# Second FFN of a hybrid decoder layer: two token parts and seven block products in place of eight

## The chip, the cores and the metric

One core of one Trainium2 chip runs the whole program. The metric is device time in microseconds: the median of the runs. In the profile, PE is TensorE (PEld its weight loads), DVE is VectorE, ACT is ScalarE, POOL is GpSimd, and SP issues most of the DMAs.

## The reference

One inference step of a decoder layer on 16 meta tokens, 1024 prompt tokens and 64 sample tokens, all in float32:

```python
x = x + 0.5 * swiglu(rmsnorm(x, g1), w1, w3, w2)      # first FFN
x = x + mix(rmsnorm(x, g)) @ w_out                    # three recurrent groups
x = x + 0.5 * swiglu(rmsnorm(x, g2), w1b, w3b, w2b)   # second FFN
y = rmsnorm(x, g_final)                               # meta tokens are dropped

def swiglu(x, w1, w3, w2):
    return (silu(x @ w1) * (x @ w3)) @ w2             # 1024 -> 2816 -> 1024
```

## The kernel before

The residual x lies with features on partitions (8 blocks of 128) and tokens along the free dimension, in three token blocks of 336, 384 and 384 columns. The second FFN leaves out the 16 meta tokens, so its blocks have 320, 384 and 384. A float32 product is made of three products of the engine's reduced float32 form: `split` (L102 to L104) rounds a tensor to a high part on ACT (L103) and subtracts it on DVE for the low part (L104), and `gemm3` (L187) sums high x high, low x high and high x low in PSUM.

`ffn` goes over the 22 slices of 128 hidden features in pairs. For each slice and token block it makes the products with w1 and w3 (8 feature blocks x 3 terms, 24 matmuls each), multiplies by 1/rms (L221, L223), applies tanh and the gate (L222 to L225), splits the result (hh, hl), and then adds the product with w2 into the residual (matmul L247, DVE L249). Weights are loaded on SP in 512 KB pieces (L177) and split by `wload`.

Three phases follow each other: the input and the first FFN, the mixing, and from L1272 the second FFN with the final norm. In the mixing, the residual lies in DRAM; `w_out` of blocks 0 and 1 is part of it. Phase 3 begins with the loads of these two blocks (L1282), their scaling and splitting (`xsplit`, L124 and L125) and the sums of squares (`square`: ACT L138, POOL L139). Then w_out of block 2 is issued (matmul L187 into pwo, DVE L1290), and after it block 2 is prepared in the same way. `rsq` (L106 to L114) is 1/sqrt by some ten small DVE operations, and `rstd_bc` spreads it over partitions (L164, L165, L167).

In the last pair of slices `turn` transposes the residual (L1309, L1310), and `finish` makes the w2 products with tokens on partitions (512 columns, L1329), adds (DVE L1331), squares (ACT L1333), multiplies by the final gain (POOL L1334), applies 1/rms (ACT L1349, DVE L1351) and stores; it runs block by block between the products of that pair. Each engine works off its instructions in an order fixed at build time by a scheduler; the order of issue in the code is its priority.

## Time and profile before

| | us |
|---|---|
| median of 3 runs (2209.11 to 2211.9) | 2211.64 |
| the profiled execution, span from first to last instruction | 2210.2 |
| PE busy | 2154.1 |
| DVE busy | 1258.3 |
| ACT busy | 675.9 |
| POOL busy | 110.1 |

Busy time is the union of an engine's instructions; the granted TensorE clock has a mean of 0.990 of its full rate over the span. A stretch is to be read by itself: the shares above are means over the three phases.

### The profile page before, as it was taken

Reading aid. Unit: us, or ns where it says so; the run is one execution under the profiler, and the core shown is the slowest. Engines: PE = TensorE matmul, PEld = TensorE weight load, DVE = VectorE, ACT = ScalarE, POOL = GpSimd, SP = SyncE. Lnnn points to the kernel's source line nnn. Section 1 sums busy time; section 2 is a strip of 40 time slices with the busy share of each in tenths; the row PEclk is TensorE's granted clock in tenths of the full one; section 3 lists DMA queues with packets and bytes.
Section 4 is the critical chain, followed back from the end, with each engine's and each line's share of the span. In section 5 each row is a group of like instructions: output and inputs, shape, how many; then the busy total and the mean of one; then the engine's idle time right before and its main releaser. Section 6 shows DMA issues by size and latency. Waiting matters only on the chain.

```text
span 2210.2 us, 32814 instructions
## 1 busy us (share of the span) xinstructions
PE 2154.1 (97%) x13190; PEld 2102.0 (95%) x13190; DVE 1258.3 (57%) x2841; ACT 675.9 (31%) x1356; POOL 110.1 (5%) x176
## 2 busy tenths in 40 slices
PE   8999999999999999999998899999999999999996
PEld 7999999999999999978997798999999999999995
DVE  7444545454444467766687886654445444444537
ACT  6221111111111144645646664311111111111214
POOL 3000000000000021000000001300000000000004
PEclk9999999999999999999999999999999999999998
DMA  6011111111111125544344346211111111111202
GB/s 180 29 48 39 54 33 48 48 48 39 48 48 39 39 71 154 131 136 137 105 104 108 84 120 198 65 39 48 48 39 58 30 57 49 39 39 48 67 1 81
DMA packets 224875, 154.56 MB, mean 70 GB/s; under 512 B 40671, under 2 KB 210180, under 8 KB 224212
## 3 DMA queue, kind: packets, MB, share of 16 engines
q1 hardware_dynamic: 219932, 150.70, 23.3%
q10 hardware_dynamic: 4792, 1.78, 0.4%
q8 instruction: 103, 1.69, 0.3%
q14 instruction: 48, 0.39, 0.1%
HBM read 123.22 MB, written 29.22 MB: 69 GB/s over the span
## 4 chain that ended last, share of the span: by engine, by line
PE 89%; DVE 5%; ACT 3%; DMA 3%; issue 1%; SPq 0%; DVEq 0%; ACTq 0%
PE p L187 47%; PE p L247 22%; PE pw L187 9%; PE pwo L187 3%; PE pq L552 1%; PE pA L754 1%; DVE sl L125 1%; ACT sh L124 1%; PE p L1329 1%; PE pgt L466 0%; DVE x L249 0%; DVE rsy L114 0%; DMA sh<-in_x_prompt_dram 0%; DMA x<-xspill 0%; PE xps L1309 0%
## 5 line engine op out<-in xcount | busy, mean ns | idle before, releaser
L249 DVE SCALAR_TENSOR_TENSOR x<-p,x 128x384 f32<-128x384 f32 (+2 forms) x504 | 265.2, 536 | 304.0 <-PE p L247 302.1
L187 PE MATMUL p<-sh,whi 128*128 128x384 f32 (+2 forms) x2112 | 403.5, 329 | 0.4 <-ACT sh L124 0.4
L187 PE MATMUL p<-sl,whi 128*128 128x384 f32 (+2 forms) x2112 | 403.4, 328 | 0.0
L187 PE MATMUL p<-sh,wlo 128*128 128x384 f32 (+2 forms) x2112 | 400.6, 328 | 0.0
L187 PEld LDWEIGHTS p<-sh,wlo 128*128 128x128 f32 x2112 | 359.0, 188 | 0.0
L187 PEld LDWEIGHTS p<-sh,whi 128*128 128x128 f32 x2112 | 356.5, 188 | 1.7 <-ACT sh L124 1.4
L187 PEld LDWEIGHTS p<-sl,whi 128*128 128x128 f32 x2112 | 357.1, 188 | 0.2
L247 PE MATMUL p<-hh,whi 128*128 128x384 f32 (+2 forms) x1008 | 331.7, 329 | 1.9 <-DVE x L249 1.8
L247 PE MATMUL p<-hh,wlo 128*128 128x384 f32 (+2 forms) x1008 | 331.8, 329 | 0.0
L247 PE MATMUL p<-hl,whi 128*128 128x384 f32 (+2 forms) x1008 | 331.3, 329 | 0.0
L103 ACT CAST whi<-wraw 128x1024 fp32r<-128x1024 f32 x168 | 176.2, 1049 | 394.7 <-PE p L247 242.2
L103 ACT CAST hh<-h 128x336 fp32r<-128x336 f32 (+1 forms) x132 | 65.8, 498 | 535.4 <-DVE h L225 479.2
L104 DVE TENSOR_TENSOR wlo<-wraw,whi 128x1024 fp32r<-128x1024 f32 x168 | 205.2, 1221 | 23.3 <-ACT whi L103 19.9
L223 DVE TENSOR_TENSOR t<-p,rb 128x336 f32<-128x336 f32 (+1 forms) x132 | 71.0, 538 | 222.0 <-PE p L187 221.9
L247 PEld LDWEIGHTS p<-hh,whi 128*128 128x128 f32 x1008 | 189.7, 188 | 2.8 <-DVE x L249 2.7
L247 PEld LDWEIGHTS p<-hh,wlo 128*128 128x128 f32 x1008 | 189.3, 188 | 0.0
L247 PEld LDWEIGHTS p<-hl,whi 128*128 128x128 f32 x1008 | 189.3, 188 | 0.0
L222 ACT ACTIVATE h<-t 128x336 f32<-128x336 f32 (+1 forms) x132 | 67.4, 511 | 334.3 <-DVE t L221 334.3
L221 DVE TENSOR_TENSOR t<-p,rb 128x336 f32<-128x336 f32 (+1 forms) x132 | 70.8, 536 | 142.5 <-PE p L187 136.4
L104 DVE TENSOR_TENSOR hl<-h,hh 128x336 fp32r<-128x336 f32 (+1 forms) x132 | 71.2, 539 | 49.6 <-ACT hh L103 49.1
L187 PE MATMUL pw<-sh,whi 128*128 128x384 f32 (+1 forms) x480 | 99.2, 338 | 0.1
L187 PE MATMUL pw<-sh,wlo 128*128 128x384 f32 (+1 forms) x480 | 98.4, 337 | 0.0
(415 smaller groups left out, 2301.6 us busy)
## 6 DMA issues: line engine op xcount, KB each, us to landing
wraw<-in_ffn_w_dram SPq DMA_DIRECT2D x132, 512.0 KB
wraw<-in_w_in_dram SPq DMA_DIRECT2D x16, 512.0 KB
wraw<-in_w_out_dram SPq DMA_DIRECT2D x16, 512.0 KB
xspill<-x SPq DMA_DIRECT2D x2, 1536.0 KB
x<-xspill SPq DMA_DIRECT2D x2, 1536.0 KB
sl<-in_x_prompt_dram SPq DMA_DIRECT2D x5, 512.0 KB
wP<-m_minus_b SPq DMA_DIRECT2D x8, 256.0 KB
qk<-z_qk SPq DMA_DIRECT2D x8, 256.0 KB
```

Source lines behind the costliest of these rows:

```text
L103: S.copy(hi, x)
L104: V.tensor_tensor(lo, x, hi.bitcast(F32), OP.subtract)
L124: S.mul(hi[:, k, :n], X[:, k, :n], vc(gname, k))
L125: V.scalar_tensor_tensor(lo[:, k, :n], X[:, k, :n], vc(gname, k), hi[:, k, :n].bitcast(F32), OP.mult, OP.subtract)
L187: PE.matmul(p, wsl(ww, k), xsl(xx, k), start=i == 0, stop=i == tot - 1)
L221: V.tensor_tensor(t1, p1[:, :n], rb[b], OP.mult)
L222: S.activation(h, t1, AF.Tanh, scale=0.5)
L223: V.tensor_tensor(t3, p3[:, :n], rb[b], OP.mult)
L247: PE.matmul(p[:, :n], w[:, g, :], x[:, :n], start=i == 0, stop=i == 3 * GRP - 1)
L249: V.scalar_tensor_tensor(X[b][:, d, :n], p[:, :n], 0.25, X[b][:, d, :n], OP.mult, OP.add)
L552: PE.matmul(p[:96, h, :m], wt[:, kb, sl, 0:96], cm[:, kb, :m], start=i == 0, stop=i == len(ks) - 1)
L754: PE.matmul(p[:, a], x[:, a], y[:, a], start=True, stop=True)
```

## The change

The 1088 tokens of the second FFN are worked off in two parts, of 576 and of 512 columns (`PARTS`), one after the other, each through all 22 slices, its output included; the weights are read and split once for each part. In each part the tokens are cut into two halves of n = 288 or 256 columns, the 1024 features into two halves, and a pair of slices is two blocks of hidden features. The product of this 2x2 scheme with w1, and the one with w3, is made of seven block products (`seven`, 12 matmuls of n columns each) in place of eight. For these, `operands` forms seven combinations of the normalised blocks of x once for each part, and splits each; `weights` forms seven combinations of the weight blocks for every pair (four POOL operations at L1372, seven splits). Partial sums are read out of PSUM banks a, b and c by ACT and DVE between products, while some banks go on summing. 1/rms is now part of x's operands. The w_out of block 2 is issued at the end of the mixing and goes to DRAM; SBUF of the first two phases is freed before phase 3, whose tiles take its place.

```diff
+PARTS = [(288, [(0, 64), (64, 128), (192, 128), (320, 128), (448, 128)]), (256, [(0, 128), (128, 128), (256, 128), (384, 128)])]
+PARTS = [(288, [(0, 64), (64, 128), (192, 128), (320, 128), (448, 128)]), (256, [(0, 128), (128, 128), (256, 128), (384, 128)])]
+ORDER = (1, 6, 2, 7, 5, 4, 3)
...
-
-    # ================================================================ phase 1: input and first FFN
+        w_out((2,), out01)
...
+    front.close()
     with ExitStack() as ph:
-        for b in range(2):
-            nc.sync.dma_start(X[b], xdr2[b][:, :, skip[b] : NB[b]])
-            for k in range(8):
-                xsplit(X[b], b, k, "ffn2_norm_g")
-                square(tp, X[b], b, k)
-            rstd_bc(tp, b)
-        nc.sync.dma_start(X[2], xdr[2])
-
-        def out2(b, d, p):
-            V.tensor_tensor(X[2][:, d, :], X[2][:, d, :], p, OP.add)
-
-        w_out((2,), out2)
-        for k in range(8):
-            xsplit(X[2], 2, k, "ffn2_norm_g")
-            square(tp, X[2], 2, k)
-        rstd_bc(tp, 2)
-
...
+        X = [xp.tile([128, 8, 2 * n], F32, tag=f"x{i}", name=f"x{i}") for i, (n, _) in enumerate(PARTS)]
+        nc.sync.dma_start(X[0][:, :, 0:320], xdr2[0][:, :, 16:336])
+        nc.sync.dma_start(X[0][:, :, 320:576], xdr2[1][:, :, 0:256])
+        nc.sync.dma_start(X[1][:, :, 0:128], xdr2[1][:, :, 256:384])
+        nc.sync.dma_start(X[1][:, :, 128:512], xdr2[2])
...
+            S.activation(acc, X[i][:, 0, :], AF.Square)
+            for k in range(1, 8):
+                q = tp.tile([128, 576], F32, tag="h", name="sq", bufs=3)[:, : 2 * n]
+                S.activation(q, X[i][:, k, :], AF.Square)
+                G.tensor_tensor(acc, acc, q, OP.add)
...
+            def block(fh, th):
+                t = temp()
+                for k in range(4):
+                    S.mul(t[:, k, :], X[i][:, 4 * fh + k, th * n : th * n + n], vc(gname, 4 * fh + k))
+                V.tensor_tensor(t, t, r[:, th, None, :].to_broadcast([128, 4, n]), OP.mult)
+                return t
...
+            b11, b12 = block(0, 0), block(0, 1)
+            t1 = minus(b12, b11)
+            split(*ops[1], b11)
+            b22 = block(1, 1)
+            t3 = minus(b22, b12, b12)
+            t2 = minus(b22, t1)
+            split(*ops[6], t2)
+            b21 = block(1, 0)
+            split(*ops[2], b21)
+            for p, t in ((7, t3), (5, t1)):
+                split(*ops[p], t)
+            split(*ops[4], minus(b21, t2, b21))
+            split(*ops[3], b22)
+            return ops
...
+        def weights(w, f):
+            r = []
+            for i in range(2):
+                t = wq.tile([128, 4, 256], F32, tag="raw", name="wraw", bufs=3)
+                src = w.rearrange("(k p) f -> p k f", p=128)
+                nc.sync.dma_start(t, src[:, 4 * i : 4 * i + 4, f * 128 : f * 128 + 256])
+                r.append(t)
+            a11, a21 = r[0][:, :, 0:128], r[0][:, :, 128:256]
+            a12, a22 = r[1][:, :, 0:128], r[1][:, :, 128:256]
+            def comb(x, y, op):
+                t = wq.tile([128, 4, 128], F32, tag="ws", name="ws", bufs=4)
+                G.tensor_tensor(t, x, y, op)
+                return t
+            s1 = comb(a21, a22, OP.add)
+            s2 = comb(s1, a11, OP.subtract)
+            s3 = comb(a11, a21, OP.subtract)
+            s4 = comb(a12, s2, OP.subtract)
+            u = {}
+            for p, x in zip(ORDER, (a11, s2, a12, s3, s1, a22, s4)):
+                hi = wq.tile([128, 4, 128], F32R, tag="whi", name="whi", bufs=7)
+                lo = wq.tile([128, 4, 128], F32R, tag="wlo", name="wlo", bufs=7)
+                split(hi, lo, x)
+                u[p] = (hi, lo)
+            return u
...
+        def seven(u, ops, n, y1, y2):
+            a, b, c = bank("a"), bank("b"), bank("c")
+            s = tp.tile([128, 288], F32, tag="p1", name="p1")[:, :n]
...
+                for ww, xx in ((wh, xh), (wh, xl), (wl, xh)):
                     for k in range(4):
+                        PE.matmul(
+                            t[:, :n], ww[:, k, :], xx[:, k, :], start=first and i == 0, stop=i == 11,
+                            skip_group_check=True,
+                        )
+                        i += 1
...
+            mm(a, 1, True)
+            S.copy(s, a[:, :n])
+            mm(b, 6, True)
+            add(y1[:, h2], s, b)
+            mm(a, 2, False)
+            S.copy(y1[:, h1], a[:, :n])
+            mm(b, 7, False)
+            add(y2[:, h2], s, b)
+            mm(c, 5, True)
+            add(y2[:, h2], y2[:, h2], c)
+            mm(b, 4, False)
+            add(y2[:, h1], s, b)
+            mm(c, 3, False)
+            add(y1[:, h2], y1[:, h2], c)
...
+                G.tensor_tensor(xq, xq, gb[:m, q * 512 : q * 512 + 512], OP.mult)
...
+        for i, (n, _) in enumerate(PARTS):
+            ops = operands(i, "ffn2_norm_g")
+            for f0 in range(0, NFB, 2):
+                last = f0 + 2 == NFB
+                ys_ = {}
+                for nm in ("ffn2_w1", "ffn2_w3"):
+                    u = weights(A[nm], f0)
+                    t = [lp.tile([128, 576], F32, tag=f"c{nm[-1]}{g}", name="c")[:, : 2 * n] for g in range(2)]
+                    seven(u, ops, n, *t)
+                    ys_[nm[-1]] = t
+                u2 = halves(f0)
...
+                for d in range(8):
+                    wh, wl = (t[:, :, d % 4 * 128 : d % 4 * 128 + 128] for t in u2[d // 4])
+                    for o, m in ((0, n), (n, n)) if 2 * n > 512 else ((0, 2 * n),):
+                        p = pz_("p2")
+                        c = 0
+                        for g in range(2):
+                            hh, hl = (t[:, o : o + m] for t in hs[g])
+                            for w, x in ((wh, hh), (wh, hl), (wl, hh)):
+                                PE.matmul(p[:, :m], w[:, g, :], x, start=c == 0, stop=c == 5)
+                                c += 1
+                        xs = X[i][:, d, o : o + m]
+                        V.scalar_tensor_tensor(xs, p[:, :m], 0.25, xs, OP.mult, OP.add)
+                if last:
+                    for j, (o, m) in enumerate(PARTS[i][1]):
+                        x = lp.tile([128, 1152], F32, tag="bf", name="xt", bufs=4)[:, :1024]
+                        turned(x, i, o, m)
+                        output(i, j, o, m, x)
```

The order in which the engines' queues stand changes at three places. The first is SP, where the second FFN begins. Before, the loads of blocks 0 and 1 (x_13473, x_13474) are issued ahead of the last w_out weights:

```order
L999 DMA xspill_1_82<-stg 128x384
L177 DMA wraw<-in_w_out_dram 128x8x128
L1282 DMA x_13473<-xspill_0_81 128x8x320
L1282 DMA x_13474<-xspill_1_82 128x3072
L1287 DMA x_13475<-xspill_80 128x3072
L177 DMA wraw<-in_w_out_dram 128x8x128 x2
L177 DMA wraw<-in_ffn_w_dram 128x8x128 x4
```

In the change, the parts' loads (x_13759 for part 0, x_13760 for part 1) stand behind the stores of block 2 (xspill_2, from the last w_out products), and the FFN's weights behind them:

```order
L992 DMA xspill_2_83<-stg 128x384 x2
L1283 DMA gb<-in_final_norm_g_dram 128x1024
L1285 DMA x_13759<-xspill_0_81 128x8x320
L992 DMA xspill_2_83<-stg 128x384
L1286 DMA x_13759<-xspill_1_82 128x8x256
L1287 DMA x_13760<-xspill_1_82 128x8x128
L1429 DMA w_14180<-in_ffn_w_dram 128x2x512
L1288 DMA x_13760<-xspill_2_83 128x8x384
L1365 DMA wraw<-in_ffn_w_dram 128x4x256 x3
```

The load of the first token block moved from ahead of w_out's last weights to the end of w_out.

The second is PE at the same place; pwo are w_out's sums, p and a are those of w1 and w3. Before:

```order
L187 MATMUL pwo<-sh_12405,wlo 128x384 x5
L165 MATMUL rbp<-dg,ones 128x64
L165 MATMUL rbp<-dg,ones 128x128 x2
L187 MATMUL pwo<-sh_12405,wlo 128x384 x3
L187 MATMUL p_13966<-sh_13477,whi 128x320 x8
L187 MATMUL p_13966<-sl_13478,whi 128x320 x8
```

In the change (ssp sums squares over partitions, rbp spreads 1/rms):

```order
L191 MATMUL pwo<-sh_12405,wlo 128x384 x8
L1304 MATMUL ssp<-ones,acc 128x1 x2
L1304 MATMUL ssp<-ones,acc 32x1
L1314 MATMUL rbp<-dg,ones 128x128
L1304 MATMUL ssp<-ones,acc 128x1 x2
L1304 MATMUL ssp<-ones,acc 32x1
L1314 MATMUL rbp<-dg,ones 128x128
L1314 MATMUL rbp<-dg,ones 128x32
L1397 MATMUL a<-op_13855,whi 128x288 x8
L1397 MATMUL a<-op_13855,wlo 128x288 x4
```

The products that were queued around the norm's small matmuls are gone from there: w_out, the norm of part 0, and the first product stand one after another.

The third is POOL at the boundary of the two parts. Before there was no boundary, and POOL had only sums of squares and, at the end of the program, the multiplications by the final gain:

```order
L139 TENSOR_TENSOR acc<-acc,sq 128x320 x7
L139 TENSOR_TENSOR acc<-acc,sq 128x384 x14
L1334 TENSOR_TENSOR sh_20226<-sh_20226,gb 128x512 x2
L1334 TENSOR_TENSOR sl_20227<-sl_20227,gb 128x512 x2
L1334 TENSOR_TENSOR sh_20326<-sh_20326,gb 128x512 x4
```

In the change (ws are weight combinations of the last pair of part 0, then of the first pair of part 1):

```order
L1372 TENSOR_TENSOR ws<-wraw 128x512
L1372 TENSOR_TENSOR ws<-wraw,ws 128x512
L1451 TENSOR_TENSOR xt<-xt,gb 64x512 x2
L1451 TENSOR_TENSOR xt<-xt,gb 128x512 x8
L1299 TENSOR_TENSOR acc<-acc,sq 128x512 x7
L1372 TENSOR_TENSOR ws<-wraw 128x512
L1372 TENSOR_TENSOR ws<-ws,wraw 128x512
```

The part-0 output's ten multiplications moved ahead of the sums of squares of part 1, and those ahead of its first weight combinations.

## Rows read from the trace of the kernel before

**Rows 1.** The page: head, busy shares, and the chain that ended last, by engine.
```profile
span 2210.2 us, 32814 instructions
...
PE 2154.1 (97%) x13190; PEld 2102.0 (95%) x13190; DVE 1258.3 (57%) x2841; ACT 675.9 (31%) x1356; POOL 110.1 (5%) x176
...
PE 89%; DVE 5%; ACT 3%; DMA 3%; issue 1%; SPq 0%; DVEq 0%; ACTq 0%
```

**Rows 2.** Windows: stretch, length, each engine's busy us, granted clock, DMA share, GB/s.
```profile
1500.00:1600.00 100.00, 100.00 (x606) 100.00 (x606) 48.34 (x85) 17.45 (x26) 0.00 (x0) 1.00 0.15 43
```

**Rows 3.** Timeline of PE, second FFN: start, us, line, operation, count.
```profile
1500.12 1.58 PE L187 MATMUL p<-sh,whi 128*128 128x384 f32 x8
...
1515.41 1.55 PE L187 MATMUL p<-sh,wlo 128*128 128x384 f32 x8
1516.80 0.31 PE L247 MATMUL p<-hh,whi 128*128 128x320 f32 x1
...
1519.44 1.33 PE L187 MATMUL p<-sh,whi 128*128 128x320 f32 x8
...
2171.02 0.40 PE L1329 MATMUL p<-whi,hh 128*128 128x512 f32 x1
...
2173.35 0.39 PE L1329 MATMUL p<-whi,hl 128*128 128x512 f32 x1
```

**Rows 4.** The chain near the end, in order of time: start, us, what.
```profile
2169.17 1.31 PE xps L1309 x12
...
2180.56 1.16 DVE rsa L109
2181.72 0.59 DVE sl L1331
...
2205.65 0.72 ACT sh L1349
```

**Rows 5.** Timeline of PE where the second FFN begins.
```profile
1372.80 2.90 PE L187 MATMUL pwo<-sh,whi 128*128 128x384 f32 x8 [4.09 <-ACT sh L124]
...
1394.82 0.77 PE L187 MATMUL pwo<-sh,wlo 128*128 128x384 f32 x3
1395.43 1.34 PE L187 MATMUL p<-sh,whi 128*128 128x320 f32 x8
```

**Rows 6.** The chain where the second FFN begins.
```profile
1353.87 8.89 DMA x<-xspill
```

**Rows 7.** Windows, 1370 to 1380, columns as in rows 2.
```profile
1370.00:1380.00 10.00, 7.20 (x25) 7.24 (x26) 9.39 (x13) 7.10 (x14) 3.77 (x5) 0.66 0.37 93
```

**Rows 8.** Groups by form, 1290 to the end: operation, count | busy us, mean ns | idle before.
```profile
L104 DVE TENSOR_TENSOR wlo<-wraw,whi 128x1024 fp32r<-128x1024 f32 x78 | 95.5, 1225 | 13.1 <-ACT whi L103 11.9 <-PE pwo L187 0.7 <-PE p L187 0.4
...
L249 DVE SCALAR_TENSOR_TENSOR x<-p,x 128x384 f32<-128x384 f32 x160 | 89.2, 558 | 102.1 <-PE p L247 100.8
...
L139 POOL TENSOR_TENSOR acc<-acc,sq 128x384 f32<-128x384 f32 x14 | 18.0, 1287 | 3.7 <-ACT sq L138 2.8
L1334 POOL TENSOR_TENSOR sh<-sh,gb 128x512 f32<-128x512 f32 x10 | 12.9, 1293 | 771.1 <-ACT sqf L1333 770.9
```

**Rows 9.** Timeline of DVE where the second FFN begins.
```profile
1370.97 1.21 DVE L125 SCALAR_TENSOR_TENSOR sl<-x,vec,sh 128x384 fp32r<-128x384 f32 x1
...
1373.04 0.61 DVE L125 SCALAR_TENSOR_TENSOR sl<-x,vec,sh 128x384 fp32r<-128x384 f32 x1
...
1386.14 0.74 DVE L109 TENSOR_SCALAR rsa<-rsv 128x3 int32<-128x3 int32 x1
...
1391.37 0.87 DVE L113 SCALAR_TENSOR_TENSOR rsa<-rsa,rsv 128x3 f32<-128x3 f32 x1
1392.27 0.16 DVE L114 SCALAR_TENSOR_TENSOR rsy<-rsa,rsy 128x3 f32<-128x3 f32 x1
```

**Rows 10.** Timeline of POOL in the same stretch.
```profile
1369.06 2.71 POOL L139 TENSOR_TENSOR acc<-acc,sq 128x320 f32<-128x320 f32 x2 [2.48 <-ACT sq L138]
...
1379.86 17.15 POOL L139 TENSOR_TENSOR acc<-acc,sq 128x320 f32<-128x320 f32 x13 [3.60 <-ACT sq L138]
```

More of the change, by code (lines that the diff above doesn't have):

```diff
@@ L169, in tile_step, with wload @@
     rb = {}
[L171 removed]
+    def wload(*parts, shape=[128, 8, 128]):
         raw = wp.tile(shape, F32, tag="raw", name="wraw")
@@ L191, in wunit, with ffn @@
         return wload((0, 128, w.rearrange("(k p) f -> p k f", p=128)[:, :, f * 128 : f * 128 + 128]))
-    def ffn(tp, X, w1, w3, w2, done, first=None, start=None, turn=None, finish=None, keep=None):
+    def ffn(tp, X, w1, w3, w2, done, first=None, start=None):
         GRP = 2
@@ new lines, in tile_step, with norms @@
+        nc.sync.dma_start(X[1][:, :, 0:128], xdr2[1][:, :, 256:384])
+        nc.sync.dma_start(X[1][:, :, 128:512], xdr2[2])
+        def norms(i):
+            n = PARTS[i][0]
+            r = tp.tile([128, 2, 288], F32, tag="rb", name="rb", bufs=1)[:, :, :n]
+            acc = tp.tile([128, 576], F32, tag="h", name="acc", bufs=3)[:, : 2 * n]
+            S.activation(acc, X[i][:, 0, :], AF.Square)
[3 more added lines that the diff above has]
+                G.tensor_tensor(acc, acc, q, OP.add)
+            cs = [(o, min(128, n - o)) for o in range(0, n, 128)]
+            for h in range(2):
+                ss = pz_("ssp")
+                for j, (o, m) in enumerate(cs):
+                    PE.matmul(ss[:m, j : j + 1], acc[:, h * n + o : h * n + o + m], ones[:, :1], start=True, stop=True)
+                v = tp.tile([128, 4], F32, tag="rsv", name="rsv", bufs=RB)[:, : len(cs)]
+                V.memset(v, 1.0)
+                for j, (o, m) in enumerate(cs):
+                    V.tensor_scalar(v[:m, j : j + 1], ss[:m, j : j + 1], 1.0 / D, EPS, OP.mult, OP.add)
+                y = rsq(tp, v, 128, len(cs))
+                q = pz_("rbp")
+                for j, (o, m) in enumerate(cs):
+                    d = tp.tile([128, 128], F32, tag="dg", name="dg", bufs=3)
+                    V.tensor_scalar(d[:m, :m], ident[:m, :m], y[:m, j : j + 1], None, OP.mult)
+                    PE.matmul(q[:, o : o + m], ones[:m, :], d[:m, :m], start=True, stop=True)
+                S.copy(r[:, h], q[:, :n])
+            return r
@@ new lines, in halves @@
+        def halves(f0):
+            wr = A["ffn2_w2"][f0 * 128 : f0 * 128 + 256, :].rearrange("(g p) (i c) -> i p g c", g=2, i=2)
+            out = []
+            for i in range(2):
+                raw = lp.tile([128, 2, 512], F32, tag="w2", name="w2", bufs=1)
+                lo = lp.tile([128, 2, 512], F32R, tag="w2l", name="w2l", bufs=2)
+                hi = lp.tile([128, 2, 512], F32R, tag="w2h", name="w2h", bufs=2)
+                nc.sync.dma_start(raw, wr[i])
+                split(hi, lo, raw)
+                out.append((hi, lo))
+            return out
@@ new lines, in turned, with output @@
+        def turned(x, i, o, m):
+            for q in range(2):
+                p = pz_("xps").rearrange("p (k t) -> p k t", k=4)
+                for k in range(4):
+                    PE.transpose(p[:m, k, :], X[i][:, 4 * q + k, o : o + m], ident)
+                S.copy(x[:m, q * 512 : q * 512 + 512].rearrange("p (k t) -> p k t", k=4), p[:m])
+        def output(i, j, o, m, x, add=None):
+            ss = tp.tile([128, 2], F32, tag="ssf", name="ssf", bufs=RB)[:m]
+            v = tp.tile([128, 4], F32, tag="rsv", name="rsv", bufs=RB)[:m, :1]
+            for q in range(2):
+                xq = x[:m, q * 512 : q * 512 + 512]
+                if add:
+                    add(q, xq)
+                sq = tp.tile([128, 576], F32, tag="h", name="sqf", bufs=3)[:m, :512]
+                S.activation(sq, xq, AF.Square, accum_out=ss[:, q : q + 1])
+                G.tensor_tensor(xq, xq, gb[:m, q * 512 : q * 512 + 512], OP.mult)
+            V.tensor_tensor(v, ss[:, 0:1], ss[:, 1:2], OP.add)
+            V.tensor_scalar(v, v, 1.0 / D, EPS, OP.mult, OP.add)
+            r = rsq(tp, v, m, 1)
+            if i == 0 and j == 0:
+                dst = O["y_sample"]
+            else:
+                s0 = o - 64 if i == 0 else 512 + o
+                dst = O["y_prompt"][s0 : s0 + 128, :]
+            for q in range(2):
+                h = slice(q * 512, q * 512 + 512)
+                xq = x[:m, h]
+                if q == 0:
+                    S.mul(xq, xq, r)
+                else:
+                    V.tensor_scalar(xq, xq, r, None, OP.mult)
+                nc.sync.dma_start(dst[:, h], xq)
```

149 lines of the change are left out of this document (68 added, 81 removed).

## The prediction

> **What bounds the kernel now.** I read the page's head first. Of 2210.2 us TensorE is busy 2154.1, 97%, and the chain that ended last lies on PE for 89% of the span [rows 1]. So the matmul stream is the bound, and an edit pays if it makes that stream shorter without opening holes in it. Next the windows in the middle of the second FFN, the only stage that changes: from 1500 to 1600 PE is busy 100.00 of 100 us at granted clock 1.00 (the upper level, 2.4 GHz), VectorE 48.34, ScalarE 17.45, GpSimd 0, DMA 0.15 [rows 2]. There is no hole to close; there is a second engine at half load and two nearly idle ones.
>
> What a matmul costs there is read from starts, since ends are modelled. From 1500.12 to 1516.80 run 12 groups of 8 matmuls of 384 columns: 16.68/96 = 173.7 ns each. From 1516.80 to 1519.44 run 18 of 320 columns: 146.7 ns. From 2171.02 to 2173.35 run 10 of 512 columns: 233 ns [rows 3]. Transposes, 12 in 1.31 us, cost 109 ns [rows 4]. The price follows the columns: (173.7 - 146.7)/64 = 0.42 ns each. So I take 133 ns for 288 columns, 120 for 256.
>
> The stage's PE work before, at these prices: 1056 x (173.7 x 2 + 146.7) for w1 and w3 = 521.8 us; 480 x 494.1 ns for w2 = 237.2; 108 x 0.233 = 25.1 for the last pair's w2; 72 x 0.109 = 7.8. Sum 791.9. The first product starts at 1395.43 [rows 5], so work alone would end at 2187.3; the rest to 2210.2 is the tail.
>
> **The change, term by term.** *Fewer products.* Per pair, part and matrix: 7 products x 12 matmuls, so 2 x 11 x 84 = 1848 of 288 columns (245.8 us) and 1848 of 256 (221.8). w2: 11 x 96 of 288 (140.4), 11 x 48 of 512 (123.0 with the last pair); the 72 transposes stay (7.8). Sum 738.8; I count **-53**. Multiplications fall by an eighth, but 288 and 256 columns pay the fixed ~12 ns (146.7 - 320 x 0.42) more often, hence less than an eighth of 521.8.
>
> *The start.* Before, blocks 0 and 1 were loaded, scaled and squared while w_out of block 2 was still running: their load of 8.89 us [rows 6] and their POOL sums lay under w_out, and FFN products followed the last w_out matmul directly (1394.82, then 1395.43). After, the w_out of block 2 is the end of the mixing, and L1285, the load of the first part, stands behind it on SP and reuses its memory. Everything up to the first product is now a chain with PE idle. Without the ACT work before it, w_out should end at E, about 1385: its last stretch lost 4.09 us waiting for ScalarE, about 3 at a granted clock of 0.66, and 1 or 2 to the norms' small products [rows 5, 7]. From E: load 8.9 until the first piece of X, then ScalarE's squares; seven POOL adds of 128x576. An add of 384 takes 1287 ns [rows 8], beside a busy DVE, so 576 would be 1.3 to 1.9, taken as 1.45: to E+22. rsq, the weights' POOL combinations and their splits share E+22 to E+31: of eleven small DVE operations from 1386.14 to 1392.43 every second took about 0.87 in place of 0.16, while POOL ran 13 adds without a pause [rows 9, 10]. Then dg, rbp, copy, a 1152-wide multiplication (1225 ns at 1024 [rows 8]: 1.36) and its cast (1.2): first product at E+36, 1421 instead of 1395. The other six operands still need 13 such DVE operations, 13 x 1.36 = 17.7, with the first weights' 14 subtractions at 0.69 and the first adds: about 31 us on DVE for the first pair's 22.3 us of products, so PE waits another 9 to 13. Term: 1421 - 1395.4 + 12 = **+38**; low end 23 (no lock, sums beside the load), high end 45 (every operation locked).
>
> *The boundary between the parts.* Before had none. After, PE's queue has the part-0 transposes, then ssp of part 1; POOL has ten multiplications by gb and only then the seven sums of part 1; the squares of part 1 stand on ScalarE behind the scalings of part 0, which wait for DVE's five rsq chains. Ten POOL operations at 1293 ns are 12.9 us [rows 8]; five chains of 13 small operations cost 10 us free and up to 12.9 more when POOL locks them: the chains at the old end, with 16 residual adds among them, took from 2180.56 to 2205.65 [rows 4]. Take 25 for the output, 7 for the sums left behind it, 4 for ssp, rsq and rbp, 2.3 for the first operand, about 7 for DVE's lag on the rest, less 4.4 of transposes that PE does meanwhile: **+42** (25 if the two chains overlap, 52 if not at all).
>
> *Steady state.* DVE's price per pair, part 0, start to start, 0.07 to 0.1 under the durations [rows 8]: ten partial sums of 288 at 0.46, 14 weight subtractions of 512 at 0.69, two w2 subtractions 1.22, six operations of 576 at 0.76, 16 residual adds at 0.45: 28.5 us, against PE's 35.1 (168 x 133 ns + 96 x 133 ns). Part 1: 26.0 against 31.3. So DVE goes from half to 81 to 83% busy. POOL adds 8 combinations of 128x512 at 1.28 = 10.3 us per pair, and these exclude DVE operations that read two SBUF tensors: the same operation took 1.21 us at 1370.97, while POOL's adds ran until 1371.77, and 0.61 us at 1373.04, while none ran [rows 9, 10]. If DVE yields for all of it: 38.8 against 35.1 and 36.3 against 31.3, that is 10 x (3.7 + 5.0) = 87 us. If for none: nothing. Partial sums and residual adds read PSUM, and such an operation kept 0.59 us beside a small one of 1.16 [rows 4]; only 16.7 of the 28.5 us can collide. The seven products share three bank tags of two buffers each, so a late partial sum does stop PE after some 3 to 4 us. I take about 1 us per pair, nearer to nothing: **+20**, both ends kept.
>
> ScalarE (15 us a pair: 14 casts, tanh, copies) and DMA (weights read twice, so 0.15 becomes about 0.3) stay far from their limits and are counted at nothing; their cover is PE's 31 us or more per pair, and without it a 512 KB load would cost some 2 us.
>
> *Tail.* Only four chunks remain instead of nine, none interleaved with products: **0**, between -5 and +5.
>
> Sum against the profiled run: 2210.2 - 53 + 38 + 42 + 20 = 2257.2; the runs' median lies 1.4 above that span: **about 2258 us**, slower by 2.1%. The likeliest case's own range is 2236 to 2282.
>
> **A rule weighed.** The row first: two lengths of one DVE operation, 1.21 and 0.61 us, with and without POOL [rows 9, 10]. The Trainium skill (SBUF — State Buffer, Who interferes with whom) says that the DVE and GpSimd share one port pair held as an exclusive lock; the row agrees. By the rule taken in full, POOL's combinations are simply added to DVE's time; that is rival B.
>
> **The rivals.** *B: VectorE becomes the bound.* Each POOL combination stops it in full, 87 us instead of 20: 2258 + 67 = 2325. For it: the long small operations of [rows 9]; against: over 40% of DVE's work reads PSUM, and 5 to 7 us of slack per pair. Decides where DVE's windows are 100% while PE's are below 92%. Chance 0.15.
>
> *C: faster.* The operand chain is hidden: the loads and squares overlap w_out, part 1 is prepared under part 0's last pairs. Then 38 + 42 shrink to under 53 - 20 = 33: 2185 to 2206. For it: two part-1 loads are issued long before they are needed. Against it: the written order puts part 1's POOL sums behind part 0's ten multiplications, and the load waits for the last w_out. It decides if the hole between the parts is under 15 us. Chance 0.08.
>
> *D: narrow matmuls don't get cheaper.* If 288 and 256 columns cost what 320 do: 1848 x (13.7 + 26.7) + 1056 x 13.7 = 89 us more: 2347. Against: 320 is already cheaper than 384 in proportion, and transposes of 128 columns cost 109 ns [rows 3, 4]. Chance 0.04. The Trainium skill (TensorE: Matmul & The Clock Gate, Back-to-back issue gap) gives a sustained 81 ns at 128 columns and 131 at 512; an estimate on the line between them is 102 ns for 288 and 114 for 384, by which the seven products would cost about 17 us more than the eight. Here 512 columns took 233 ns [rows 3], so the measurement decides.
>
> *E: it cancels.* Holes of 33 us or so: 2207 to 2216. Chance 0.05.
>
> **The numbers.** Forecast 0.66, B 0.15, C 0.08, D 0.04, E 0.05 and 0.02 for other slower causes. What the measurement tells from no change is about 0.2%, 4.4 us. Faster 0.08, same 0.05, slower 0.87. For 8 in 10 the range leaves out D, most of B and the lower part of C: 2222 to 2300, from the low ends of start and boundary (-15, -17) up to half of the coupling's.
>
> **What the new profile should show.** Starts of 288-column matmuls 133 ns apart, of 256 columns 120. PE empty or sparse for some 35 us before the first product, with the granted clock below 1.00 when it returns, and for some 40 us around 1830, with POOL nearly full in both. Between them PE at 94 to 98%, DVE at 80 to 95%. I am wrong if the holes are below 15 us each, if matmuls keep 147 ns, or if DVE stands at 100% in mid-part.

## The result

The changed kernel takes 2263.78 us (median of 4 runs, 2262.61 to 2263.99) against 2211.18 us of the kernel before on the same chip (median of 4): a ratio of 1.0235, 95% interval 1.022 to 1.0249. The forecast was 2258 us, slower by 2.1%. The profiled execution has a span of 2262.2 us, so the spans differ by 52.0 us.

The page of the changed kernel, head, busy shares and chain, answers to [rows 1]:

```profile
span 2262.2 us, 35535 instructions
...
PE 2118.2 (94%) x13758; PEld 2039.8 (90%) x13758; DVE 1532.1 (68%) x3207; ACT 865.6 (38%) x1701; POOL 371.4 (16%) x345
...
PE 84%; DVE 8%; ACT 3%; DMA 3%; issue 1%; POOL 1%; SPq 0%; ACTq 0%; DVEq 0%; POOLq 0%
```

PE is busy 36 us less than before, and yet the span is 52 us longer: PE has stretches without work, and the share of the chain that lies on PE falls from 89% to 84%, while that on DVE and POOL rises. The windows say where (the row from 1500 answers to [rows 2]); columns are the stretch, its length, busy us of PE, PEld, DVE, ACT and POOL, the granted clock, the DMA share and GB/s:

```profile
1400.00:1420.00 20.00, 1.21 (x6) 1.11 (x6) 12.80 (x20) 7.87 (x13) 16.14 (x12) 0.50 0.58 189
1420.00:1440.00 20.00, 9.94 (x44) 8.71 (x45) 14.47 (x31) 6.75 (x12) 4.42 (x3) 0.64 0.18 52
1440.00:1460.00 20.00, 15.99 (x83) 15.07 (x82) 18.89 (x19) 11.30 (x17) 3.63 (x2) 0.66 0.02 3
1500.00:1600.00 100.00, 100.00 (x758) 100.00 (x757) 82.07 (x137) 42.16 (x73) 36.62 (x24) 1.00 0.31 92
...
1840.00:1860.00 20.00, 8.29 (x54) 6.46 (x53) 16.65 (x48) 12.38 (x30) 9.93 (x8) 0.77 0.24 72
1860.00:1880.00 20.00, 1.01 (x4) 0.93 (x4) 11.30 (x38) 10.65 (x23) 11.52 (x9) 0.50 0.21 79
1880.00:1900.00 20.00, 11.53 (x48) 10.18 (x48) 15.50 (x33) 8.33 (x15) 2.37 (x1) 0.59 0.09 27
...
1909.00:1931.00 22.00, 20.06 (x170) 19.84 (x169) 22.00 (x30) 12.06 (x23) 10.58 (x7) 1.00 0.29 78
...
2000.00:2100.00 100.00, 100.00 (x698) 93.23 (x697) 84.70 (x131) 45.93 (x78) 36.01 (x25) 1.00 0.34 104
```

In mid-part PE is as full as before although DVE went from 48 to 82 us of 100 and POOL from 0 to 37. The loss sits in two holes, before the first product of part 0 and between the parts, and in the stretch behind each, where PE is not full yet and the granted clock, which fell to 0.50 while PE had next to nothing to do, is still below 1.00.

What a product costs, from starts on PE's timeline; answers to [rows 3]:

```profile
1503.65 1.21 PE L1397 MATMUL a<-op,whi 128*128 128x288 f32 x8
1504.71 0.69 PE L1397 MATMUL a<-op,wlo 128*128 128x288 f32 x4
...
2001.74 1.12 PE L1397 MATMUL c<-op,whi 128*128 128x256 f32 x8
2002.70 0.63 PE L1397 MATMUL c<-op,wlo 128*128 128x256 f32 x4
```

288 columns: (1504.71 - 1503.65)/8 = 132.5 ns, against 133 forecast; 256 columns: (2002.70 - 2001.74)/8 = 120 ns, as forecast. The medians of all such distances in the stage are 132, 119.5 and, at 512 columns, 228 ns. At these the stage's PE work is 1848 x (132 + 119.5) + 1056 x 132 + 528 x 228 + 72 x 109 ns = 732.4 us, 59.5 less than before. Below, "lost" in a stretch is its length minus its products at these prices.

**The start.** The chain from the last w_out product on (start, us, what); answers to [rows 5, 6]:

```profile
1386.74 8.56 DMA x<-xspill
1395.33 0.68 ACT acc L1295
...
1396.72 1.42 POOL acc L1299
...
1408.24 1.23 PE ssp L1304 x6
...
1409.80 0.99 DVE rsa L113
1410.81 1.20 DVE rsy L114
1412.04 1.20 DVE rsa L116
...
1416.23 1.14 DVE rsy L118
1417.37 1.20 DVE wlo L108 x2
1418.58 1.14 DVE rsa L116
1419.71 2.27 DVE wlo L108 x2
...
1422.29 1.20 DVE dg L1313
```

Load, squares, seven sums on POOL until 1408.2, then 12.5 us until dg, for an rsq that takes 2.4 us when POOL is idle (1878.6 to 1881.0, at the boundary). While POOL forms weight combinations, several of rsq's small operations take 1.0 to 1.2 us in place of 0.16, and weight splits (wlo, w2l) stand in between on DVE for another 6 us. The first product starts at 1429.51. What follows it, on PE's timeline:

```profile
1451.15 1.16 PE L1397 MATMUL b<-op,whi 128*128 128x288 f32 x4
1452.11 1.16 PE L1397 MATMUL b<-op,wlo 128*128 128x288 f32 x4
```

(1452.11 - 1451.15)/4 = 240 ns a product, against 132.5 above: the granted clock was 0.50, the lower level (1.2 GHz), from 1430 to 1434, behind the hole, and again from 1441.5 to 1454.5, after PE had mostly waited since 1436. What is lost in the 45 us behind a part's first product is called its lag below. Of this one's 16.0 us, 52 products at this level make up 5.7; most of the rest is PE waiting for operands, with DVE busy 18.89 of the 20 us from 1440.

**The boundary.** POOL's timeline; xt by gb is part 0's output, acc the sums of part 1:

```profile
1844.46 6.17 POOL L1451 TENSOR_TENSOR xt<-xt,gb 64x512 f32<-64x512 f32 x5 [42.38 <-ACT sqf L1450]
1853.64 1.27 POOL L1451 TENSOR_TENSOR xt<-xt,gb 128x512 f32<-128x512 f32 x1 [3.01 <-ACT sqf L1450]
1856.82 2.49 POOL L1451 TENSOR_TENSOR xt<-xt,gb 128x512 f32<-128x512 f32 x2 [1.91 <-ACT sqf L1450]
1861.22 1.27 POOL L1451 TENSOR_TENSOR xt<-xt,gb 128x512 f32<-128x512 f32 x1 [1.91 <-ACT sqf L1450]
1863.43 1.27 POOL L1451 TENSOR_TENSOR xt<-xt,gb 128x512 f32<-128x512 f32 x1 [0.94 <-ACT sqf L1450]
1864.65 1.45 POOL L1299 TENSOR_TENSOR acc<-acc,sq 128x512 f32<-128x512 f32 x1
1867.26 2.60 POOL L1299 TENSOR_TENSOR acc<-acc,sq 128x512 f32<-128x512 f32 x2 [1.16 <-ACT sq L1298]
1872.16 5.29 POOL L1299 TENSOR_TENSOR acc<-acc,sq 128x512 f32<-128x512 f32 x4 [2.30 <-ACT sq L1298]
```

The last 288-column product starts at 1841.7 and the first of 256 at 1886.25: 44.6 us, of which the output holds POOL until 1864.7, the sums take until 1877.5, and ssp, rsq, rbp and the first operand 8.8. POOL itself waits for ACT: four times for a square of the output, and the sums twice more (1.16 and 2.30), since on ACT the scaling of the output's last chunk (1870.49) stands ahead of part 1's squares from 1871.12 on.

### The profile page after: what moved, and what is told of

The parts are those of the page before. It is cut to its first block, busy times and chain, and to the rows that moved or that the text cites. A ratio compares the mean times of both kernels' runs of the same rounds, so it can differ in the third digit from the quotient of the medians.

```text
span 2262.2 us, 35535 instructions
## 1 busy us (share of the span) xinstructions
PE 2118.2 (94%) x13758; PEld 2039.8 (90%) x13758; DVE 1532.1 (68%) x3207; ACT 865.6 (38%) x1701; POOL 371.4 (16%) x345
## 4 chain that ended last, share of the span: by engine, by line
PE 84%; DVE 8%; ACT 3%; DMA 3%; issue 1%; POOL 1%; SPq 0%; ACTq 0%; DVEq 0%; POOLq 0%
PE p L191 23%; PE p L1524 11%; PE p L240 11%; PE b L1397 9%; PE pw L191 8%; PE a L1397 6%; PE c L1397 5%; PE pwo L191 4%; PE pq L545 1%; DVE sl L129 1%; PE pA L747 1%; DVE wlo L108 1%; DVE rsa L116 1%; POOL acc L1299 1%; DVE rsy L118 1%
## 5 line engine op out<-in xcount | busy, mean ns | idle before, releaser
L107 ACT CAST whi<-wraw 128x512 fp32r<-128x512 f32 (+1 forms) x234 | 188.7, 806 | 345.0 <-PE p L240 116.4
L108 DVE TENSOR_TENSOR wlo<-wraw,whi 128x512 fp32r<-128x512 f32 (+1 forms) x234 | 244.7, 1046 | 19.7 <-ACT whi L107 16.9
L191 PE MATMUL p<-sh,whi 128*128 128x384 f32 (+1 forms) x1056 | 205.3, 332 | 0.4 <-ACT sh L128 0.4
L191 PE MATMUL p<-sl,whi 128*128 128x384 f32 (+1 forms) x1056 | 203.4, 330 | 0.0
L191 PE MATMUL p<-sh,wlo 128*128 128x384 f32 (+1 forms) x1056 | 202.1, 330 | 0.0
L191 PEld LDWEIGHTS p<-sh,whi 128*128 128x128 f32 x1056 | 179.7, 189 | 1.6 <-ACT sh L128 1.4
L191 PEld LDWEIGHTS p<-sh,wlo 128*128 128x128 f32 x1056 | 180.8, 188 | 0.0
L191 PEld LDWEIGHTS p<-sl,whi 128*128 128x128 f32 x1056 | 179.8, 188 | 0.1
L1372 POOL TENSOR_TENSOR ws<-wraw 128x512 f32<-128x512 f32 x88 | 136.1, 1546 | 258.3 <-DMA wraw<-in_ffn_w_dram 170.5
L240 PE MATMUL p<-hh,whi 128*128 128x384 f32 (+1 forms) x528 | 174.3, 330 | 1.9 <-DVE x L242 1.8
L240 PE MATMUL p<-hh,wlo 128*128 128x384 f32 (+1 forms) x528 | 174.2, 330 | 0.0
```

The source lines that it names most:

```text
L107: S.copy(hi, x)
L108: V.tensor_tensor(lo, x, hi.bitcast(F32), OP.subtract)
L191: PE.matmul(p, wsl(ww, k), xsl(xx, k), start=i == 0, stop=i == tot - 1)
L240: PE.matmul(p[:, :n], w[:, g, :], x[:, :n], start=i == 0, stop=i == 3 * GRP - 1)
L1372: G.tensor_tensor(t, x, y, op)
```

## The experiments

Each was timed once on a chip on which the kernel before was timed too, unless rounds are named. On the chip of the first four the kernel before took 2215.45 us, on the others 2209.4 to 2210.5; spans are set against 2262.2 us of the changed kernel, and what is below 5 us across chips is not read.

**Eight products in place of seven, the rest as changed.**

```diff
-            s1 = comb(a21, a22, OP.add)
...
-            for p, x in zip(ORDER, (a11, s2, a12, s3, s1, a22, s4)):
+            for p, x in zip(ORDER, (a11, a12, a21, a22)):
```

> The two parts stay, but each pair's product with w1 or w3 is made of eight block products (24 matmuls summed in one bank, copied out by ScalarE), so there are four operands and four weight splits in place of seven, no combinations and no partial sums. Theory (the seven products do shorten PE's stream; what is lost lies in the two stretches without products): 1 x 12 x 2 x 11 x (132 + 120 ns) = 67 us more matmuls, less lag behind the operands at both places (about -10 each) and a shorter wait of the first product (-6): about 2304 us, PE still 100% in mid-part. Rival (the scheme's combinations, splits and partial sums cost more than its products save): below 2264 us.

2292.6 us, span 2290.5: 11 us under the theory, and far from the rival. The diff shows only the weights; there are also four operands in place of seven, and copies by ACT in place of the partial sums. Per part 264 more products, 264 x (132 + 119.5) ns = 66.4 us. The losses of the changed kernel less those here: before the first product 43.2 - 39, in the 45 us after each first product 16.0 - 2.2 and 16.0 - 1.8, at the end of part 0 10.8 - 5.6, between the parts 39.6 - 41: together 36 us given back, so 30 net, and 28 by the spans. Two parts, narrower products and a late start are the loss; the seven-product scheme by itself earns, but 36 of its 66 us are lost again, 28 of them behind the first products.

**No combinations of weights on POOL.** The kernel leaves out these sums and takes plain blocks.

```diff
-            s1 = comb(a21, a22, OP.add)
-            s2 = comb(s1, a11, OP.subtract)
-            s3 = comb(a11, a21, OP.subtract)
-            s4 = comb(a12, s2, OP.subtract)
+            s1, s2, s3, s4 = a21, a22, a11, a12
```

> The four GpSimd combinations of weight blocks per matrix and pair are left out, the split of a plain weight block stands in their place (the output is no longer the reference's); everything else is issued as before. Theory (PE, not VectorE, sets the pace in mid-part): PE 100% there as before, only the start loses some of its blocked small operations: 2254 to 2260 us. Rival (GpSimd's lock on VectorE is what the parts cost): 2225 us or less.

2247.01 us, span 2245.3: 7 us under the theory's range, 22 above the rival's. The same stretch of part 0 here and in the changed kernel, whose products come 11 us later, and the split of a weight block on DVE (count, busy us, mean ns of one), here and there:

```profile
1469.00:1779.00 310.00, 310.00 (x2345) 310.00 (x2344) 227.18 (x423) 126.99 (x218) 0.00 (x0) 1.00 0.29 91
```
```profile
1480.00:1790.00 310.00, 309.99 (x2342) 309.76 (x2341) 259.03 (x425) 127.77 (x217) 114.60 (x76) 1.00 0.31 91
```
```profile
L108 DVE TENSOR_TENSOR wlo<-wraw,whi 128x512 fp32r<-128x512 f32 x308 | 209.5, 691 | 21.7 <-ACT whi L107 18.2 <-PE a L1394 3.0 <-issue 0.3
```
```profile
L108 DVE TENSOR_TENSOR wlo<-ws,whi 128x512 fp32r<-128x512 f32 x176 | 143.9, 823 | 1.5 <-ACT whi L107 1.3
...
L1372 POOL TENSOR_TENSOR ws<-wraw 128x512 f32<-128x512 f32 x88 | 136.1, 1546 | 258.3 <-DMA wraw<-in_ffn_w_dram 170.5 <-DVE wlo L108 48.2 <-DVE x L1527 22.2
```

The combinations cost DVE 259.03 - 227.18 = 31.9 us, 28% of POOL's 114.6, and PE nothing: it is full with and without. So the gain lies where a part begins: 8 us less are lost behind w_out (35.2 for 43.2), and the two lags are 14.1 and 14.0 for 16.0 each. Another 3 of the 17 us are not the edit's: w_out itself ends 3 us sooner, as it does in several kernels below with their combinations in place. No cost in mid-part was there to be taken away.

**The start alone**: the first token part is loaded into memory of its own, its norm is issued ahead of w_out of block 2, and w_out adds straight into X.

```diff
+        r0 = norms(0)
+        w_out((2,), out2)
+        front.close()
+        lp, op_, wq = pool("l3"), pool("o3"), pool("w3")
```

> x of both parts is given SBUF of its own, loaded before w_out of block 2 is issued, part 0's norm is computed under w_out, and w_out adds block 2 straight into x of part 1. Theory (44 us from w_out's end to the first product are a chain of load, sums, rsq that only its place in the order exposes): the first product follows w_out by 2 to 5 us, w_out itself may end up to 8 us later because ScalarE now works for both, the lag behind the operands (16 us) stays: 2225 to 2238 us. Rival (the chain is limited by the engines' work, which then only slows w_out): above 2250 us.

2242.46 us, span 2240.7: 21 us of the start's 50, 4 us short of the theory's range. From w_out to the first product only 2.9 us are lost, but w_out itself ends at 1408.4, 23 us later, above all since its first sum waits for the load of the residual that it adds into:

```profile
1376.32 2.93 PE L191 MATMUL pwo<-sh,whi 128*128 128x384 f32 x8 [11.75 <-DVE x L1288]
...
1398.37 1.64 PE L191 MATMUL pwo<-sh,whi 128*128 128x384 f32 x8 [2.07 <-DVE x L1288]
```

**The same, that residual loaded first** (its load ahead of the other three on SP).

> As the early start, but the piece of x that w_out adds into is loaded first and not last. Theory (of w_out's 23 us delay there, 12 are one wait for that load): 2228 to 2236 us. Rival (the loads and the norm's work slow w_out in any order): above 2239 us.

2241.78 us, span 2240.0, no better, as the rival had it. That wait fell to 3.29 us, and the next in SP's order took its place in the chain: w_out's last weights, and behind them the norm of part 0.

```profile
1371.41 8.21 DMA wraw<-in_w_out_dram
```

**The boundary alone**: the norm of part 1 before pair 9 of part 0, part 0's output after pair 4 of part 1.

```diff
+                if i == 0 and f0 == 16:
+                    rr = norms(1)
...
+                if i == 1 and f0 == 6:
+                    for j, (o, m) in enumerate(PARTS[0][1]):
...
+                        output(0, j, o, m, x)
```

> Part 1's norm is issued before the ninth pair of part 0, and part 0's output (transposes, squares, rsq, scaling, stores) after the fourth pair of part 1. Theory (42 us between the last w2 product of part 0 and the first product of part 1 are output and norm in a chain): the gap falls to 3 to 6 us, the lag behind the operands (14 us) stays, the output's 65 small VectorE operations cost 2 to 6 us inside part 1: 2225 to 2236 us. Rival (VectorE is so full in part 1 that the output's work only moves and stops PE there): above 2250 us.

2253.02 us, span 2251.1: 11 us off where 28 to 38 were expected, and so the rival's range. The hole is gone (the first 256-column product starts at 1800.7, beside part 0's w2 products), but PE loses 24 to 28 us between 1800 and 1860, and 20 where the output now stands, in two waits above all:

```profile
2030.18 1.97 PE L1438 MATMUL xps<-ident,x 128*128 128x128 f32 x8 [5.08 <-ACT xt L1439]
2043.64 2.08 PE L1396 MATMUL a<-op,whi 128*128 128x256 f32 x8 [11.49 <-ACT c L1411]
```

ACT's copies out of the banks (c, which PE's next products need) are queued behind the output's scalings, and those wait for the rsq chain.

**The output one chunk per pair**, pairs 3 to 7, otherwise as the last one.

> As the one before (part 1's norm early), but part 0's five output chunks are issued one behind each of pairs 3 to 7 of part 1, not together. Theory (the 20 us lost at one place in part 1 are VectorE's and ScalarE's queues, in which a partial sum stands behind a whole chain of small operations): 2232 to 2242 us. Rival (the output costs VectorE the same wherever it stands, since VectorE is full): 2247 us or more.

2253.63 us, span 2251.9, the rival's range again: each chunk costs PE 3 to 8 us, in sum about what they cost together. Spreading this work out did not make it cheaper.

**Start and boundary together** (residual first, early norm, output chunk by chunk).

> Early start with that load first, early norm of part 1, and part 0's output spread. Theory (the two places are independent): the savings add to about 57 us: 2200 to 2213 us. Rival (the scheduler, or VectorE, gives part of one back when the other is gone): above 2220 us.

2221.6 us, span 2219.7. The time is in the rival's range, though not for the rival's reason: the 42 us are more than the 22 and 10 of the two apart, so neither gain was given back. W_out ends at 1386.7 here, at 1392.1 with the start alone (residual first); 3.5 of these us are there already at w_out's first product (1204.5 for 1208.0), ahead of all that was edited, and the rest was not followed up. The part-0 lag (16.4 us) and the output's cost stay.

**The same, in the first pair of each part the w1 and w3 products in turns**, so that one operand serves twice as many products; 3 rounds.

```diff
+                    runs.append(seven(u, ops, n, *t))
...
+                while runs:
+                    runs = [r for r in runs if next(r, 0) is None]
```

> As the one before, and in the first pair of each part the seven products with w1 alternate with the seven with w3, so that each operand feeds 24 matmuls (3.2 us) when it is ready, not 12. Theory (the 13 to 16 us behind each first product are PE waiting for an operand that takes VectorE about 3 us, while only 1.6 us of products can use it): both lags fall to 3 to 6 us: 2184 to 2199 us, faster than the kernel before. Rival (VectorE's total work up to the end of the first pair, about 35 us against 22, sets the lag): no more than 4 us less than the one before.

2227.83 us (2225.25 to 2230.49), ratio to before 1.0077 (1.006 to 1.0094). No gain, as the rival had it: the lags are 16.7 and 16.1 us, for 16.4 and 14.5 in the one before. In the profiled run some 3 us of what it takes more are there already at w_out's first product. So the lag is set by the work that the first pair needs, not by the order in which PE asks for it.

**Two rsq chains instead of five for part 0's output.**

```diff
+                    for js in ([0, 1, 2], [3, 4]):
...
+                        output(i, js, xs)
```

> The changed kernel with one edit: at the boundary the five chunks of part 0's output share two chains of rsq (three columns, two columns) in place of five chains. Theory (the output's length there is set by VectorE's 65 small operations, each second one behind a GpSimd multiplication): 39 fewer of them at about 0.3 us: 2248 to 2254 us. Rival (ScalarE's copies and squares, 10 x 0.58 and 10 x 0.8 us, and GpSimd's ten multiplications set it): 2258 us or more.

2262.53 us, span 2260.8, the rival's range; the loss between the parts is 39.8 (39.6 in the changed kernel). The number of small operations is not what the output takes. Where its time goes, in DVE's and POOL's timelines:

```profile
1848.41 4.92 DVE L1456 TENSOR_TENSOR rsv<-ssf 128x3 f32<-128x3 f32 x1 [5.34 <-ACT sqf L1454]
```
```profile
1843.48 9.84 POOL L1455 TENSOR_TENSOR xt<-xt,gb 64x512 f32<-64x512 f32 x8 [44.92 <-ACT sqf L1454]
```

An addition of 128x3 took 4.92 us: it ended at 1853.33, when POOL's eight multiplications ended (1853.32). In the changed kernel the same happened to the first chain (4.33 us from 1846.31, POOL until 1850.63).

**The output of part 0 last of all**, the norm of part 1 left at the boundary. This separates the two.

```diff
-                if last:
-                    for j, (o, m) in enumerate(PARTS[i][1]):
...
+        for j, (o, m) in enumerate(PARTS[0][1]):
...
+            output(0, j, o, m, x)
```

> The changed kernel, but part 0's output is issued after part 1's, at the end of the program; the norm of part 1 stays at the boundary. Theory: between the parts TensorE waits mainly for the output of part 0, which stands ahead of part 1's squares on ScalarE and ahead of its sums on GpSimd; the norm alone needs seven sums (9 us) and the 9 us from the first ssp product to the first product of part 1. From the last 288-column product to the first of 256 columns it is then 10 to 22 us in place of the 44.6 of the changed kernel, and the lag of the operands behind it stays at about 14 us. The 25 us or so of output come back at the end, so the total is about 2259 us (2250 to 2272). Rival: the norm's own chain takes the time, and the gap stays at 35 us or more; the total is then 2275 or more.

2251.99 us, span 2250.3, in the theory's range. From the last 288-column product (1843.4) to the first of 256 there are 8.7 us, and 8.0 are lost instead of 39.6. POOL's and PE's timelines:

```profile
1829.62 8.15 POOL L1299 TENSOR_TENSOR acc<-acc,sq 128x512 f32<-128x512 f32 x6
```
```profile
1852.09 1.23 PE L1397 MATMUL a<-op,whi 128*128 128x256 f32 x4 [2.79 <-ACT op L107]
```

With nothing ahead of them, part 1's squares and sums run under the last w2 products of part 0. At the end of the program the output costs 17.6 us (34.2 lost from 40 us before PE's last instruction on, 16.6 in the changed kernel), and the end of part 0 3.4 more. This is less than the theory's 25 or so, and the gap is smaller than its 10 to 22.

**Two chains, and a buffer of its own for the fifth chunk.**

```diff
+                        if 4 in js:
+                            xs.append(op_.tile([128, 2, 1024], F32, tag="op3", name="xt")[:, 0])
```

> The kernel with two rsq chains at the boundary, with a fifth buffer for the fifth chunk of part 0's output (in the memory of an operand that part 0 no longer needs). Theory: with two chains as with five, the fifth chunk's copy out of PSUM waited for the store of the first chunk, whose buffer it takes, and part 1's squares and sums stand behind that chunk on ScalarE and GpSimd. With its own buffer its copy comes at 1850 in place of 1860, POOL's ten multiplications end at about 1857, the sums of part 1 at about 1866, and the first product of part 1 some 10 us earlier: a gap of 30 to 34 us in place of 44, span 2249 to 2253 in place of 2260.8, a time of about 2252.5 us. Rival: the buffer sets nothing, since the same queues hold the same work; gap over 41, time 2260 or more.

2256.95 us, span 2255.2, between the two theories: the gap is 41.1 us (1838.4 to 1879.5) against 44.9 with two chains and four buffers. The fifth copy came at 1848.1, the last multiplication ended at 1858.6 for an expected 1857, and the sums, expected to end at 1866, at 1870.7. DVE's and POOL's timelines:

```profile
1846.09 6.15 DVE L1456 TENSOR_TENSOR rsv<-ssf 128x3 f32<-128x3 f32 x1 [5.35 <-ACT sqf L1454]
```
```profile
1841.15 11.07 POOL L1455 TENSOR_TENSOR xt<-xt,gb 64x512 f32<-64x512 f32 x9 [42.42 <-ACT sqf L1454]
1857.34 1.27 POOL L1455 TENSOR_TENSOR xt<-xt,gb 128x512 f32<-128x512 f32 x1 [5.12 <-ACT sqf L1454]
1858.57 2.61 POOL L1299 TENSOR_TENSOR acc<-acc,sq 128x512 f32<-128x512 f32 x2
```

The last chunk's second square stands on ACT behind three scalings (from 1854.71), which wait for the rsq chain, whose first addition (6.15 us) ended when POOL's nine multiplications did (1852.22). So the buffer is worth some 4 us, and ACT's queue kept the rest.

**Start, boundary and output together, with further edits**: residual in two pieces, w_out's weights on ACT's DMA queue, operands' temporaries in memory of their own, early norm, output in two groups with one chain each; 3 rounds.

```diff
+        nc.sync.dma_start(X[1][:, 0:3, 128:512], xdr[2][:, 0:3])
...
+        w_out((2,), out2, nc.scalar)
...
+                if i == 1 and f0 in (6, 12):
...
+                    output(0, js, xs)
```

> Early start in another order (a third of block 2's residual, then x of part 0, then the rest), w_out's weights on ScalarE's DMA queue so that they don't stand behind 6 MB of other loads, the operand temporaries in SBUF of their own, early norm of part 1, part 0's output in two groups with one rsq chain each behind pairs 4 and 7 of part 1. Theory (the start still loses 36 us to queues: a load behind loads, sums behind combinations; the output 23 us to chains): start 36 to 15 or 20, output 23 to 10 or 13: 2188 to 2206 us, faster than the kernel before. Rival (the work of VectorE and GpSimd at the start and in part 1 is what PE waits for, in any order): 2214 us or more.

2217.45 us (2214.01 to 2220.05), ratio 1.0031 (1.002 to 1.0042): in the rival's range, the best version, and still slower than before by 0.3%. W_out now ends at 1387.2 and the first product comes at 1392.4, but the FFN's weights, whose memory belongs to w_out's phase until then, are first issued at 1387.37, and 26.8 us are lost in the 45 behind the first product (6.6 of them in products at the lower clock, 0.50 from 1390 to 1427). PE's and POOL's timelines there:

```profile
1392.39 2.29 PE L1405 MATMUL a<-op,whi 128*128 128x288 f32 x8 [3.58 <-ACT whi L107]
...
1420.03 2.29 PE L1405 MATMUL b<-op,whi 128*128 128x288 f32 x8 [7.33 <-ACT op L107]
```
```profile
1401.16 12.85 POOL L1380 TENSOR_TENSOR ws<-wraw 128x512 f32<-128x512 f32 x1 [2.60 <-DVE w2l L108]
```

This combination took 12.85 us where the one before it took 1.26. DVE worked off twelve splits, sums and scalings without a pause meanwhile (1401.06 to 1412.89), and the combination ended 1.1 us after them: here it is POOL that is held up, and what it forms is in the chain to the product at 1420.03.

## Why the forecast held, and where its terms were off

The forecast, slower by 2.1% for two holes in the matmul stream, was right in direction and mechanism: the stage's PE work fell, the parts' middles stayed full, and the two holes cost more than the products saved. The terms, forecast and measured:

| term | forecast | measured | from |
|---|---|---|---|
| fewer products | -53 | -59.5 | 732.4 against 791.9 at the prices above |
| start | +38 | +50 | first product 34.1 later (1429.5 for 1395.4), 16.0 lost in the 45 us after it |
| boundary | +42 | +56 | 39.6 lost between the parts, 16.0 in the 45 us after |
| steady state | +20 | +10 | 10.8 at the end of part 0; mid-part 1.4 and -1.9 |
| tail | 0 | -6 | 16.6 lost against 2210.2 - 1395.4 - 791.9 = 22.9 |

The measured terms sum to +50, the spans say +52.0. That the sum came closer than its terms was luck: misses of +12 and +14 met misses of -6, -10 and -6. Besides, the boundary's own terms (25 + 7 + 4 + 2.3 + 7 - 4.4) add to 40.9 and not to 42.

*Prices of the products* were right to 1 ns at 288 and 256 columns, which refutes rival D.

*The start* was right up to the ssp product (1408.2, E + 23 for E + 22). Too small was "E+22 to E+31" for rsq, combinations and splits: they took until E + 37. The step named the splits but gave them no size, and they alone took 6 us among rsq's operations on DVE. Without the combinations 8 us less are lost behind w_out. From dg to the first product it was 7.2 us for 5. The lag was 16.0 for a forecast of 9 to 13: about 10 us of waiting, as forecast, and about 6 in products at the lower clock, which the forecast saw coming as a sign but gave no price. The clock alone does not set the lag: in the last experiment the granted clock was 1.00 in all but some 3 us of part 1's first 45, and 14.3 are lost there. It is set by the work of forming operands and weights, on DVE above all: the products in turns did not move it, and with eight products, four operands and no sums it is 2, behind a hole almost as long (39 us).

*The boundary* had its order right and three sizes wrong: output 23 us for 25, sums 12.8 for 7, from ssp to the first product 8.8 for 6.3, lag 16.0 for 7, again with some 6 at the lower clock. "DVE's five rsq chains" was the wrong thing to count: two chains take as long. Shown is that the output ahead of the norm makes the hole: without it 8.0 us are lost. Of the sums' 12.8 us, 9.3 are the seven operations and 3.5 the two waits for ACT behind the output's scalings. That these scalings are late because POOL holds DVE's small operations is read from the traces of three kernels (small operations of 4.33, 4.92 and 6.15 us, each to the end of a run of POOL's multiplications); a kernel in which POOL doesn't multiply by gb was not tried.

*The steady state* was the term with the widest bounds, 0 to 87, and the row nearer to zero decided, as taken; but the 1 us a pair was not there. DVE ran at 82 to 85% in mid-part with PE at 100.00. Rival B's sign, DVE at 100% and PE below 92%, is not seen there; it is seen behind the second hole, late in the lag (22.00 and 20.06 of the 22 us from 1909). The Trainium skill (SBUF — State Buffer, Who interferes with whom) has VectorE and GpSimd share a port pair as an exclusive lock, and excepts VectorE's operations with at most one input from SBUF, outside its 2-port modes. The trace agrees with both: from 1480 to 1790 the residual adds, which read PSUM, took 451 ns with POOL at work beside them (63 of them) and 451 without (68), the weight splits, with two inputs from SBUF, 1209 (43) and 682 (89). POOL is held up too: combinations took 1546 ns, multiplications of the same size 1293 before [rows 8]. So the forecast's reason, that much of DVE's work reads PSUM, is borne out, though not by the row that it was read from: at that 0.59 us (2181.72 [rows 4]) POOL stood still, its multiplication having ended at 2181.70. What was 10 us is the end of part 0, where w2 products of the last pairs stand back to back and wait for residual adds and for the last casts and splits of the gated products (hh, hl); the sum had no term for it.

*The signs.* The prices, the two holes and the clock below 1.00 behind them came as forecast. POOL was nearly full in the first hole only (16.14 of 20 us from 1400; 9.93 and 11.52 of 20 in the second), and between the holes PE was at 100%, not at 94 to 98.

*Rival C*, a hidden chain, did not happen in the changed kernel and was tried by hand. Each edit gained less than the hole that it removed: 21 of 50 at the start, 11 of 56 at the boundary. Of the price of hiding, what was seen is a load that now waits behind others on SP, ACT's bank copies behind output work, memory that is free too late, and a combination that DVE held up. The best version leaves the scheme 7 to 8 us slower than before; its 59.5 us of saved products are not enough for the holes that remain. Whether better placement of the first weights would bring it below the kernel before stays open.

## What to carry to other kernels

A product scheme that saves an eighth of the multiplications pays at most what the matmul stream shortens by; the operands that it forms in advance are a serial chain on DVE, ACT and POOL each time the stream begins anew, so count the beginnings first. A stage split in two has a second beginning: issue the next part's norm ahead of the first part's output, or the in-order queues put the output's work in front of it (39.6 us lost, 8.0 with the output elsewhere). Price the output where it goes as well: it cost some 20 us inside part 1 and 17.6 at the end, so that moving it gained only 10 to 12 in all. When a chain is hidden, look for the queue that it now stands in, since several of the edits here moved the wait instead of removing it.

## Not expected of the hardware

Small DVE operations can wait out a whole run of POOL operations and not only one: 4.92 us for an addition of 128x3, until POOL's eight multiplications were over, and 6.15 us until nine were. At other times such an operation took 1.0 to 1.2 us beside POOL work, and the next ones 0.16. It goes the other way too: one POOL combination took 12.85 us while twelve DVE operations on SBUF tensors ran without a pause. In full mid-part stretches the same neighbours cost DVE 28% of POOL's time, since its operations that read PSUM did not stretch at all (451 ns with and without). What decides which engine gets through first was not tried.
